# Layer 0's shifts and scales computed on the matmul array, and layer 1's modulation vectors moved from head 0 to heads 1 to 3

## The chip, the cores and the metric

One core of a Trainium2 chip runs the program. A core has five engines that work side by side and meet through semaphores: TensorE (PE in the rows, the matmul array, with its weight loads as PEld), VectorE (DVE), ScalarE (ACT), GpSimd (POOL) and SyncE (SP, which here only issues DMAs). The metric is the device time of one execution in microseconds (us); less is better.

## What is computed

A two-layer backbone over 512 latent tokens and 256 context tokens, 1024 features wide. Each layer is a normalised, modulated, gated residual step:

```
mod = silu(c) @ ada_w[i] + ada_b[i]          # shift, scale, gate: 3 x 1024, one set for c, one for c_ctx
h   = rms_norm(x, norm_g[i]) * (1 + scale) + shift
x   = x + gate * mixer(h)
```

The mixer of layer 0 is a bidirectional chunkwise mLSTM with four heads: projections to q, k (256 each per head), v, o, z (512 each per head) and four gates per head, a decay-weighted attention, a division by a denominator, `sigmoid(o) * normed * silu(z)`, and an output projection. The mixer of layer 1 is windowed attention over a band of 128 positions and the context. Layer 0 needs shift, scale and gate for both `c` (latent tokens) and `c_ctx` (context tokens); layer 1 needs shift and scale for both and the gate for `c` alone.

## The kernel before

Features lie on the 128 partitions (eight blocks j of 128) and tokens run along the free dimension (512 latent, then 256 context). Every large product is made in fp32r with operands split into a rounded part and a remainder (`hi`, `lo`), in three passes: `whi`x`hi`, `whi`x`lo`, `wlo`x`hi`. The rounded part comes from a ScalarE copy, the remainder from a subtraction on VectorE or GpSimd (`split`, L107).

The program's phases, in order of time:

- **Start.** 36 matmuls on zeros while x is loaded (`warm`), squares on ScalarE and their sums over the array (`pst`), and `rstd` (`rs`, L268).
- **The loop over the eight blocks j** (L313 to L371). For each block x is multiplied by `rstd` (L348, GpSimd), the modulation is applied by ScalarE (`enter`, L285: Identity with a scale and a bias per partition, which it reads from `modc`), the result is split into `HL` and `HC` (L288 on ScalarE, L289 on GpSimd), and TensorE then adds the block's share to the q and k of head 0 (`pqk`) and to all gates (`pgate`). So j's matmuls need j's shift and scale in `modc`.
- **Where shift and scale come from before.** `dots` (L206) multiplies a 128x1024 block of `ada_w` by silu(c) or silu(c_ctx), both broadcast over the partitions in `c2`, and sums along the row: one VectorE instruction for each block, part and vector, then a read of the accumulator. The eight scales and the shifts of blocks 0 and 4 to 7 are made so; the shifts of blocks 1 to 3 are made on the array (L328, then three transposes, L337).
- **Head 0.** Scores (`psc`), the gates' scans on VectorE (`gates`, L391 to L431), then the projections o and z (`po`, `pz`) interleaved with the decay weights and denominators (`decay`: L497 to L567, with `pden` at L520) and with modulation vectors (`mods`), in an order written by hand in the string `HEAD0`: o is a step of o and z, d a step of the decay, m one modulation vector. Then v (`v_proj`, `pv`), and the attention product (`ppv`).
- **Modulation vectors in head 0.** `todo` lists 32 vectors: layer 0's gate (8 blocks), then layer 1's shift, scale and gate (24). Each loads 512 KB and makes two dots (one for layer 1's gate). For the first eight the dot with `c_ctx` is a GpSimd multiplication (L210) and a ScalarE sum (L211). All 32 are done in head 0.
- **Heads 1 to 3** repeat q, k, scores, gates' weights, v, attention and o and z, with head h-1's output projection (`pwo`) between. In these heads o and z run last, from the end of `ppv`.

Tiles come from pools of fixed buffers; a new tile waits for the last reader of the buffer that it takes over. Within what the code and its `issue_after` marks fix, a scheduler sets each engine's order; each engine then works strictly in that order.

Of the kernel before, what the change touches and what calls it, by code (L numbers as in the profile page):

```python
# [16 lines left out]
P = 128  # L17
# [48 lines left out]
def hybrid_kernel(ctx: ExitStack, tc: tile.TileContext, a: dict, out: bass.AP, dbg=None):  # L68
# [50 lines left out]
    c2 = vga[:, 0:2048].rearrange("p (v k) -> p v k", v=2)  # L119
    crow = t0([P, 1792], F32, "pb")  # L120
    stage = [vga[:, 2048:3072]] + [vgb[:, 1024 * i : 1024 * i + 1024] for i in range(3)]
    qkp = t0([P, 6144], F32, "qkp")
    stage += [qkp[:, 1024 * i : 1024 * i + 1024] for i in range(2)] + [t0([P, 1024], F32, "qkt")]
    loaded = [0]

    def ada0(j, part):
        st = stage[loaded[0] % 7]
        loaded[0] += 1
        sy.dma_start(st, a["ada"][0, j, :, part])
        return st  # L130

    ccol = t0([P, KT, 2], F32, "ccol")
# [4 lines left out]
    small = [(crow[32 * v : 32 * v + 1, 0:D], a["cc"][v : v + 1]) for v in range(2)]  # L137
    small += [(ccol, a["cct"]), (adab, a["adab"]), (ng, a["ng"]), (hg, a["hg"]), (gb, a["gb"])]

    def load_x(small=()):  # L140
        xs = [t_([P, 4, T], F32, n) for n in ("xa", "xb")]
        for j in range(KT):
            sy.dma_start(xs[j // 4][:, j % 4], a["xin"][:, j])
            for dst, src in small[:2] if j == 0 else small[j + 1 : j + 2]:
# [4 lines left out]
    st0 = [ada0(0, 1), ada0(0, 0)]  # L149
# [9 lines left out]
    make_identity(nc, ident)  # L159
    tiny = t0([P, 1], F32, "tiny")  # L160
# [45 lines left out]
    def dots(layer, part, j, src, c2, vecs=(0, 1), pool=()):  # L206
        r = None
        for v in vecs:
            if v in pool:
                ge.tensor_mul(src, src, c2[:, v])  # L210
                se.activation(src, src, AF.Copy, accum_out=modc[:, layer, part, j, v : v + 1])  # L211
                continue
            junk = t0([P, 1024], BF16, "junk", 1)
            r = ve.tensor_tensor_reduce(
                out=junk, in0=src, in1=c2[:, v], scale=1.0, scalar=0.0,
                op0=ALU.mult, op1=ALU.add, accum_out=modc[:, layer, part, j, v : v + 1])
        return r
# [27 lines left out]
    for js in ((0, 1, 2, 3), (4, 5), (6, 7)):  # L245
        for j in js:
            q = tmp()
            lastsq = se.activation(q, x[j], AF.Square)
            if j == 1:
                for v in range(2):  # L250
                    r = crow[32 * v : 32 * v + 1, 0:D]
                    se.activation(r, r, AF.Silu)
                    ge.partition_broadcast(c2[:, v], r, channels=P)
            if j == 3:
                se.activation(ccol, ccol, AF.Silu)
# [7 lines left out]
    with after(*lastadd):  # L263
        lastdot = ve.tensor_scalar(bp1, adab[:, :, 1], 1.0, None, op0=ALU.add)
# [7 lines left out]
    with after(lastdot):  # L272
        dots(0, 1, 0, st0[0], c2, (0,))
        mod_fix(0, 1, 0, (0,))
        dots(0, 0, 0, st0[1], c2, (0,))
        mod_fix(0, 0, 0, (0,))
    rstd_exp, rstd_done = rs(0, TL, lastsq)
    xr_0 = tmp()
    xr0 = ve.tensor_mul(xr_0[:, 0:TL], x[0][:, 0:TL], rstd[:, 0:TL])
# [3 lines left out]
    def enter(j, v, xr, hf):  # L283
# [4 lines left out]
        hi = se.copy(dst[:, 0, j], hf[:, l:r])  # L288
        (ge if j or v else ve).tensor_sub(dst[:, 1, j], hf[:, l:r], f32(dst[:, 0, j]))  # L289
        return hi  # L290

    hf_0 = tmp()
    hi_0 = enter(0, 0, xr_0, hf_0)
    with after(xr0, hi_0):
        rs(TL, T)
        ve.tensor_mul(xr_0[:, TL:T], x[0][:, TL:T], rstd[:, TL:T])
        dots(0, 1, 0, st0[0], c2, (1,))
        mod_fix(0, 1, 0, (1,))
        dots(0, 0, 0, st0[1], c2, (1,))
        mod_fix(0, 0, 0, (1,))  # L300

    wgt = t0([P, 2048], F32R, "s")
# [3 lines left out]
    with after(rstd_exp):  # L306
        split(raw, wgt[:, 0:1024], wgt[:, 1024:2048], se, ge)
    half = big("pshift")
    acc = [big("pqk") for _ in range(3)]
    pg = ch("pgate")  # L310
    wq = [[None, None], [None, None]]
    stn = []
    for j in range(KT):  # L313
        if j == 0:
            for k in range(4):
                stn.append(qkp[:, 2048 + 1024 * k : 2048 + 1024 * k + 256 * NJ].rearrange("p (k c) -> p k c", k=2))
                sy.dma_start(stn[k], a["adan"][k])
        if j % 4 == 0:
            for u in range(2):
                with after(rstd_exp, *([xr0] if j or u else [])):  # L320
                    wq[u][j // 4] = load_w(a["w0"][0, u, j // 4], None if j or u else ge,
                                           raw=t0([P, 1024], F32, "pb") if u and not j else None)
        if j == 0:
            with after(laststat):
                warm(half, WARM2)

            for k in range(KT):
                te.matmul(half[0:2, 0 : P * NJ], ccol[:, k], stn[k // 2][:, k % 2], start=(k == 0), stop=(k == KT - 1))  # L328
            rows = t0([P, TL], F32, "bc1")
            with after(xr0):  # L330
                dots(0, 1, 1, ada0(1, 1), c2, (0,))
                lastdot = dots(0, 1, 1, stage[(loaded[0] - 1) % 7], c2, (1,))
                mod_fix(0, 1, 1)
            with after(rstd_exp):
                se.copy(rows[0:2, 0 : P * NJ], half[0:2, 0 : P * NJ])
                for i in range(NJ):
                    te.transpose(half[:, TL + 2 * i : TL + 2 * i + 2], rows[0:2, i * P : (i + 1) * P], ident[0:2, 0:2])  # L337
            with after(lastdot):
                for i in range(NJ):
                    ve.tensor_scalar(modc[:, 0, 0, 1 + i], half[:, TL + 2 * i : TL + 2 * i + 2],  # L340
                                     adab[:, 0, 0, 1 + i : 2 + i], None, op0=ALU.add)
        for part in (1, 0) if j > NJ else (1,) if j > 1 else ():
            with after(xr0):
                dots(0, part, j, ada0(j, part), c2)
                mod_fix(0, part, j)
        if j:
            xr, hf = tmp(), tmp()
            ge.tensor_mul(xr, x[j], rstd)  # L348
            enter(j, 0, xr, hf)
            enter(j, 1, xr, hf)  # L350
        else:
            enter(0, 1, xr_0, hf_0)
        st, sp = j == 0, j == KT - 1
        hl, hc = hparts(j)
        wgj = (wg[0][:, j], wg[1][:, j])
        wj = [[[wq[u][j // 4][m][:, j % 4, f * P : (f + 1) * P] for m in range(2)] for f in range(2)] for u in range(2)]
        mm3((pg[:, 0:TL],), wgj, [hl], st, sp)
# [3 lines left out]
        if j == 0:  # L361

            for u in range(2):
                with after(laststat):
                    te.matmul(acc[2][:, u * TL : (u + 1) * TL], zeror, wgt[:, 0:TL], start=True, stop=False)
        for u in (1, 0):
            for f in range(2):
                for i, (wi, m) in enumerate(PASSES):
                    te.matmul(acc[2][:, u * TL + f * TC : u * TL + (f + 1) * TC], wj[u][f][wi], hc[m],
                              start=False, stop=sp and f == 1 and i == 2)  # L370
        mm3((pg[:, TL:T],), wgj, [hc], st, sp)  # L371
# [11 lines left out]
    evac(1, True)  # L383

# [213 lines left out]
    def v_proj(h, vv):  # L598
# [9 lines left out]
        for c in range(4):  # L608
            w = ws[c]
            for n in range(6):  # L610
# [4 lines left out]
                if c == 3:  # L615
                    split(acc[n], vv[0][:, n], vv[1][:, n])
            if c < 2:
# [108 lines left out]
    vgb = t0([P, 3072], F32, "vgb")  # L726
    stage = [vga[:, 2048:3072]] + [vgb[:, 1024 * i : 1024 * i + 1024] for i in range(3)]

    def mods(n):
        for _ in range(min(n, len(todo))):  # L730
# [4 lines left out]
            dots(layer, part, j, st, c2, range(nv), pool=(1,) if len(todo) > NPOOL else ())  # L735

    def mods_fix():
        for layer, part, nv in ((0, 2, 2), (1, 0, 2), (1, 1, 2), (1, 2, 1)):
# [5 lines left out]

    xa = t_([P, 4, T], F32, "xa")
# [18 lines left out]
    stage = [vga[:, 2048:3072], t0([P, 1024], F32, "pb")]  # L764
    vgb = t0([P, 3072], F32R, "vgb")
    vv = [t_([P, 6, 512], F32R, "xb"), vgb.rearrange("p (t e) -> p t e", t=6)]
    vp = v_proj(0, vv)
    for n in MV:
        next(vp)
        mods(n)  # L770
    run(vp)
    mods(len(todo))
    H, norm = pv(vv, *pl, s)

    def gate0():
# [8 lines left out]
        mods_fix()  # L784


    for h in range(1, NH0):
# [13 lines left out]
        next(vp)  # L801
        next(dec)
# [14 lines left out]
        run(o_z(h, gated, pre, lambda: normalise(*norm)))  # L817
# [407 lines left out]
def layout(inp):  # L1225
# [74 lines left out]
```

## Time and profile before

| | |
|---|---|
| median of three runs | 1245.92 us (1245.25 to 1247.76) |
| the profiled execution | 1247.21 us |
| its span, first to last instruction | 1245.4 us |
| mean granted TensorE clock | 0.971 of full speed |
| PE busy | 1159.6 us, 93% |
| DVE / ACT / POOL busy | 820.4 / 548.8 / 304.8 us |

The profiled execution takes 1.3 us more than the median, and 1.8 us of it lie outside the span. PE is the engine with the least room: 86 us of the span are without a matmul, and a clock of 0.971 means that it ran at half speed for some part of the rest. The busy shares by slice show both losses mostly in the first quarter of the span: there the digits of PE are 7 and 8, behind it 9.

### The profile page before, as it was taken

The numbers are of one execution on the slowest core, as the hardware profiler recorded it, in microseconds if no ns is written. First come the engines' busy times: TensorE is split into PE (matmuls) and PEld (weight loads), VectorE is DVE, ScalarE is ACT, GpSimd is POOL, SyncE is SP. The second block draws the span as 40 slices with busy tenths as digits, with TensorE's granted clock in tenths as the row PEclk, the third lists the DMA queues.
The fourth block names the chain that finished last, engine by engine and source line by source line (L and its number), as shares of the span: only waits on it lengthen the run. The fifth ranks groups of instructions, "written<-read, shape, count | busy, mean of one in ns | idle before, by whom it ended". The sixth has DMA issues, their size and how long they took to land. (4 is left out here: it accounts for less than half of the span.)

```text
span 1245.4 us, 15926 instructions
## 1 busy us (share of the span) xinstructions
PE 1159.6 (93%) x6213; PEld 976.1 (78%) x6213; DVE 820.4 (66%) x1203; ACT 548.8 (44%) x913; POOL 304.8 (24%) x235
## 2 busy tenths in 40 slices
PE   7778698899999999999999999999999799998997
PEld 4666587687877888877888887788999587877776
DVE  6979798978672533366163148254777478989876
ACT  6324552333433422333423234343475377766663
POOL 3860770014301200420120222020043213223220
PEclk9788899999999999999999999999999899999999
DMA  8411643564211112121022211103205914124002
GB/s 305 169 51 34 203 130 115 158 217 161 87 54 34 49 67 68 64 76 51 18 81 68 68 47 64 51 20 121 81 20 119 220 51 119 56 81 122 32 18 68
DMA packets 38000, 112.71 MB, mean 90 GB/s; under 512 B 5027, under 2 KB 9251, under 8 KB 37413
## 3 DMA queue, kind: packets, MB, share of 16 engines
q1 hardware_dynamic: 35108, 104.35, 25.8%
q0 software_dynamic: 2816, 7.34, 3.4%
q8 instruction: 49, 0.80, 0.3%
q14 instruction: 27, 0.21, 0.1%
HBM read 103.42 MB, written 8.26 MB: 90 GB/s over the span
## 5 line engine op out<-in xcount | busy, mean ns | idle before, releaser
L103 ACT CAST whi<-wraw 128x1024 fp32r<-128x1024 f32 x102 | 106.9, 1051 | 198.3 <-PE pwo L189 43.8
L109 POOL TENSOR_TENSOR wlo<-wraw,whi 128x1024 fp32r<-128x1024 f32 x32 | 81.0, 2538 | 249.9 <-ACT whi L103 239.8
L109 DVE TENSOR_TENSOR wlo<-wraw,whi 128x1024 fp32r<-128x1024 f32 x70 | 89.2, 1275 | 60.9 <-ACT whi L103 60.7
L189 PE MATMUL pz<-HL,whi 128*128 128x512 f32 x256 | 96.3, 399 | 0.0
L189 PE MATMUL po<-HL,whi 128*128 128x512 f32 x256 | 96.0, 399 | 0.0
L189 PE MATMUL pqk<-HL,whi 128*128 128x512 f32 x256 | 94.3, 408 | 0.2 <-ACT whi L103 0.2
L189 PE MATMUL pv<-whi,HL 128*128 128x512 f32 x256 | 86.4, 405 | 5.1 <-DVE vgb L109 2.8
L189 PE MATMUL pz<-HC,whi 128*128 128x256 f32 x256 | 72.1, 282 | 0.0
L189 PE MATMUL po<-HC,whi 128*128 128x256 f32 x256 | 72.0, 281 | 0.0
L641 POOL TENSOR_TENSOR tmp<-tmp,tmp 128x768 f32<-128x768 f32 x8 | 15.9, 1984 | 228.4 <-ACT tmp L640 228.4
L189 PEld LDWEIGHTS pv<-whi,HL 128*128 128x128 f32 x256 | 49.8, 196 | 17.4 <-DVE vgb L109 4.2
L189 PE MATMUL Lq<-HL,whi 128*128 128x512 f32 (+1 forms) x192 | 56.1, 372 | 6.0 <-DVE szt L1068 6.0
L189 PEld LDWEIGHTS pqk<-HL,whi 128*128 128x128 f32 x256 | 49.9, 195 | 13.1 <-ACT whi L103 0.7
L189 PE MATMUL pqk<-HL,wlo 128*128 128x512 f32 x128 | 53.6, 419 | 6.9 <-DVE wlo L109 5.1
L1136 PE MATMUL Lpv<-PT,V 128*128 128x512 f32 x144 | 54.3, 431 | 5.7 <-DVE PT L109 4.5
L189 PEld LDWEIGHTS pz<-HL,whi 128*128 128x128 f32 x256 | 48.8, 190 | 12.4
L189 PEld LDWEIGHTS po<-HL,whi 128*128 128x128 f32 x256 | 48.5, 190 | 12.3
L1101 DVE TENSOR_REDUCE negm<-Lsc 128x2 f32<-128x1024 f32 (+1 forms) x32 | 43.4, 1355 | 15.7 <-PE Lsc L1099 15.2
L189 PE MATMUL pqk<-HC,whi 128*128 128x256 f32 x192 | 53.6, 279 | 0.0
L109 DVE TENSOR_TENSOR PT<-LT,PT 128x512 fp32r<-128x512 f32 x72 | 48.9, 684 | 4.8 <-ACT PT L103 4.2
L109 DVE TENSOR_TENSOR qkp<-pqk,qkp 128x768 fp32r<-128x768 f32 (+2 forms) x20 | 15.8, 794 | 54.7 <-ACT qkp L103 54.7
L189 PE MATMUL pz<-HL,wlo 128*128 128x512 f32 x128 | 51.7, 404 | 0.0
(386 smaller groups left out, 3399.1 us busy)
## 6 DMA issues: line engine op xcount, KB each, us to landing
wraw<-w SPq DMA_DIRECT2D x84, 512.0 KB, 3.6
wraw<-wo SPq DMA_DIRECT2D x24, 512.0 KB, 3.6
vga<-ada SPq DMA_DIRECT2D x16, 512.0 KB, 3.7
vgb<-ada SPq DMA_DIRECT2D x15, 512.0 KB, 4.9
pb<-ada SPq DMA_DIRECT2D x9, 512.0 KB, 3.7
Q<-hl POOLq DMA_DIRECT2D x8, 512.0 KB, 6.3
xa<-xin SPq DMA_DIRECT2D x8, 384.0 KB, 4.6
xb<-xin SPq DMA_DIRECT2D x8, 384.0 KB, 5.3
```

The lines of the kernel that those rows point to most:

```text
L103: se.copy(dst, src)
L109: return (le or ve).tensor_sub(lo, src, f32(hi))
L189: te.matmul(o, w[s], mv[m], start=first and i == 0, stop=last and i == 2)
L641: (ge if e < 3 else ve).tensor_add(ss, ss, sq)
L1101: ve.tensor_reduce(nmx[:, 0, 2 * p2 : 2 * p2 + 2], both, axis=AX.X, op=ALU.max, negate=True)
L1136: te.matmul(po, V[:, kb, g], hl[:, m], start=(bi == 0 and m == 0), stop=(bi == len(blocks) - 1 and m == 1))
```

## The change

Layer 0's shifts and scales all come from the array (`mod_quarter`): one quarter is 256 features of shift and of scale, that is two blocks j. `ada_w`'s part is laid out on the host as `ada0`, 16 loads of 512 KB. Each quarter is eight fp32 matmuls of 32 columns of weights and 512 moving columns, four of them in the array's four groups of 32 columns (output partitions 0, 32, 64, 96), the second four added on top. ScalarE copies the result, four tiny matmuls with the selector `sel2` add the four groups and turn the rows into columns, and three small VectorE operations add the bias and the norm's gain.

```
+    def mod_quarter(R, srcs, c):
+        for kk in range(2):
+            for g in range(4):
+                te.matmul(R[32 * g : 32 * g + 32], ccol[:, 4 * kk + g], srcs[4 * kk + g], start=kk == 0, stop=kk == 1)
+        rt = tmp()[:, 0:TL]
+        se.copy(rt, R)
+        for q in range(4):
+            te.matmul(R[:, 2 * q : 2 * q + 2], rt[:, q * P : (q + 1) * P], sel2, start=True, stop=True)
...
     for j in range(KT):
+        if j % 2 and j < KT - 1:
+            c = j // 2 + 1
+            with after(lastmm):
+                mod_quarter(R[:, c % 2 * TL : c % 2 * TL + TL], st0[c], c)
+        xr, hf = tmp(), tmp()
+        ve.tensor_mul(xr, x[j], rstd)
+        enter(j, 0, xr, hf)
+        enter(j, 1, xr, hf)
...
-        mm3((pg[:, 0:TL],), wgj, [hl], st, sp)
...
+    pg = ch("pgate")
+    for j in range(KT):
+        mm3((pg[:, 0:TL], pg[:, TL:T]), (wg[0][:, j], wg[1][:, j]), hparts(j), j == 0, j == KT - 1)
```

The multiplication by `rstd` and the subtractions of `HL` and `HC` are on VectorE now, and GpSimd has nothing to do in the loop. The gates' matmuls stand behind the loop. 36 and 8 warming matmuls (36 and 10 before); the eight stand among the statistics.

In head 0 only layer 0's gate remains, with both dots on VectorE. The 24 vectors of layer 1 are done in heads 1 to 3, in the stage of o and z:

```
-HEAD0 = "ooodommoommmmmomoddmmmmm"
-MV = (0, 2, 2, 3, 3)
-NPOOL = 24
+HEAD0 = "ooodommommommommodd"
+MODS = (None, (3, 3, 2, 2), (3, 3, 2, 2), (4, 0, 0, 0))
...
+    def mods_at(rows, slots):
+        nonlocal c2, stage
+        c2 = rows.rearrange("p (v k) -> p v k", v=2)
+        sy.dma_start(rows, c_d.rearrange("r k -> (r k)").partition_broadcast(P))
+        stage = slots
...
+        rows = t0([P, 6144], F32, "qkp")
+        mods_at(rows[:, 0:2048], [rows[:, 1024 * i : 1024 * i + 1024] for i in range(2, 6)])
+        for n, _ in zip(MODS[h], o_z(h, gated, pre, lambda: normalise(*norm))):
+            mods(n)
+    mods_fix((1, 0, 2), (1, 1, 2), (1, 2, 1))
```

`c2` now comes from DRAM: silu(c) is turned into rows on the array, written out (`c_d`) and read back by every partition, 1 MB each time, for head 0 and again for each of heads 1 to 3. In heads 1 to 3 the vectors' buffers are the q and k buffer `qkp`, which `ppv` has to have read first.

**TensorE, between block 0 and block 1.** `R` is the accumulator of the quarters, `tmp_313` its copy, `pqk_222` the context part of q and k. Before:

```order
L369 MATMUL pqk_228<-HC_202,whi_236 128x256 x2
L369 MATMUL pqk_228<-HC_202,wlo_237 128x256
L189 MATMUL pgate_229<-HC_202,s_220 128x256 x3
L189 MATMUL pgate_229<-HL_201,s_220 128x512 x3
L189 MATMUL pqk_226<-HL_201,whi_236 128x512 x2
```

Now:

```order
L331 MATMUL pqk_222<-HC_218,whi_234 128x256 x2
L331 MATMUL pqk_222<-HC_218,wlo_235 128x256
L221 MATMUL R_199<-vgb_67,ccol_71 32x512 x4
L221 MATMUL R_199<-qkp_68,ccol_71 32x512 x4
L225 MATMUL R_199<-sel_109,tmp_313 128x2 x4
L192 MATMUL pqk_220<-HL_217,whi_234 128x512
L192 MATMUL pqk_221<-HL_217,whi_240 128x512
```

Block 1's first matmul stands directly behind the second quarter, with nothing between them; the third quarter stands so behind block 2, and the fourth behind block 4, there with nine of the gates' matmuls behind it.

**GpSimd, in head 0's decay.** `tmp_805` and `tmp_791` gather the sums for the denominator that `pden` waits for. Before:

```order
L537 COPY tmp_805<-pb_798 128x128
L535 TENSOR_TENSOR tmp_805<-pb_798 128x512
L536 TENSOR_TENSOR tmp_805<-pb_798,s_734 128x128
L210 TENSOR_TENSOR vgb_796<-vgb_796,vga_66 128x1024
L545 TENSOR_TENSOR tmp_805<-tmp_805,s_734 128x128
L545 TENSOR_TENSOR tmp_805<-tmp_805,s_734 128x256
L210 TENSOR_TENSOR vgb_796<-vgb_796,vga_66 128x1024
L545 TENSOR_TENSOR tmp_805<-tmp_805,s_734 128x384
L546 TENSOR_TENSOR tmp_805<-tmp_805,pb_798 128x512
```

Now:

```order
L508 COPY tmp_791<-pb_784 128x128
L506 TENSOR_TENSOR tmp_791<-pb_784 128x512
L507 TENSOR_TENSOR tmp_791<-pb_784,s_718 128x128
L516 TENSOR_TENSOR tmp_791<-tmp_791,s_718 128x128
L516 TENSOR_TENSOR tmp_791<-tmp_791,s_718 128x256
L516 TENSOR_TENSOR tmp_791<-tmp_791,s_718 128x384
L517 TENSOR_TENSOR tmp_791<-tmp_791,pb_784 128x512
```

The modulation's multiplications (L210) no longer stand between the sums.

**VectorE, in head 1's stage of o and z.** `wlo` is the remainder of half a unit of weights, `junk` the unused product of a dot. Before:

```order
L810 SCALAR_TENSOR_TENSOR pb_2872<-pb_2872,s_2186 128x768 x2
L109 TENSOR_TENSOR wlo_3132<-wraw_3129,whi_3131 128x1024
L689 SCALAR_TENSOR_TENSOR tmp_3068<-tmp_3068,pz_3019 128x768
L814 SCALAR_TENSOR_TENSOR tmp_3068<-tmp_3068,hg_74,pb_2872 128x768
L109 TENSOR_TENSOR vgb_2531<-tmp_3068,vga_2530 128x768
L109 TENSOR_TENSOR wlo_3138<-wraw_3135,whi_3137 128x1024
```

Now:

```order
L785 SCALAR_TENSOR_TENSOR pb_2751<-pb_2751,s_2063 128x768 x2
L212 ISA junk_3031,modc_113<-qkp_2749 128x1024
L212 ISA modc_113 128x1
L106 TENSOR_TENSOR wlo_3041<-wraw_3038,whi_3040 128x1024
L662 SCALAR_TENSOR_TENSOR tmp_2962<-tmp_2962,pz_2913 128x768
L212 ISA junk_3034,modc_113<-qkp_2749 128x1024
L212 ISA modc_113 128x1
L789 SCALAR_TENSOR_TENSOR tmp_2962<-tmp_2962,hg_74,pb_2751 128x768
L212 ISA junk_3036,modc_113<-qkp_2749 128x1024
L212 ISA modc_113 128x1
L106 TENSOR_TENSOR vgb_2408<-tmp_2962,vga_2407 128x768
L106 TENSOR_TENSOR wlo_3047<-wraw_3044,whi_3046 128x1024
```

The rows of the remainders now have dots between them: since the stage began, ten stand ahead of the first of these two and twelve ahead of the second, where there were none.

## Rows read from the trace of the kernel before

**Rows 1.** Busy time in stretches: stretch, length, us and (times) by engine, PEclk.
```profile
140.00:160.00 20.00, 8.61 (x35) 7.24 (x34) 19.96 (x19) 7.27 (x12) 17.77 (x10) 0.66 0.40 126
...
sum 320.00, PE 272.36 PEld 221.64 DVE 273.37 ACT 128.93 POOL 129.32; mean PE 17.02 PEld 13.85 DVE 17.09 ACT 8.06 POOL 8.08
```

**Rows 2.** ACT's waits, 0 to 100 us: line, releaser, total, times, longest.
```profile
ACT tmp L285 <- DVE modc L224: 25.4, 4, 8.3
ACT tmp L285 <- DVE modc L222: 11.9, 3, 6.6
```

**Rows 3.** PE's waits, 0 to 400 us, same columns.
```profile
PE pden L520 <- ACT tmp L103: 13.8, 2, 11.4
...
PE pv L189 <- DVE xb L689: 3.5, 2, 2.3
...
PE pv L189 <- DVE vgb L109: 2.8, 1, 2.8
PE psc L189 <- ACT qkp L103: 2.8, 2, 2.2
...
PE pwo L189 <- DVE vgb L109: 1.6, 2, 1.2
```

**Rows 4.** Two lines' instructions: duration in ns (min/median/max), first and last start.
```profile
L328 PE MATMUL pshift<-qkp,ccol x16: 485/486/486, 19.7 to 24.5; 128*2 128x384 f32 x16
...
L214 DVE CUSTOM_DVE_ANT_0 junk<-vgb,vga x25: 1211/1226/3307, 17.2 to 191.7; 128x1024 bf16<-128x1024 f32 x25
```

**Rows 5.** Groups in the loop, 30 to 96 us: shapes, count, total, mean ns.
```profile
L285 ACT ACTIVATE tmp<-tmp,modc 128x512 f32<-128x512 f32 x7 | 5.7, 815 | 37.3 <-DVE modc L224 25.4 <-DVE modc L222 11.9
L288 ACT CAST HL<-tmp 128x512 fp32r<-128x512 f32 x7 | 4.2, 603 | 0.0
```

**Rows 6.** TensorE's timeline: start, length, instruction, idle before and its releaser.
```profile
71.20 0.79 PE L189 MATMUL pqk<-HL,wlo 128*128 128x512 f32 x1 [4.24 <-DVE wlo L109]
...
95.34 0.52 PE L189 MATMUL pgate<-HC,s 128*128 128x256 f32 x3
...
111.67 0.39 PE L189 MATMUL po<-HL,whi 128*128 128x512 f32 x1
111.90 0.28 PE L189 MATMUL po<-HC,whi 128*128 128x256 f32 x1
112.01 0.40 PE L189 MATMUL po<-HL,whi 128*128 128x512 f32 x1
...
115.20 0.87 PE L435 MATMUL pgt<-ident,vgb 64*128 64x64 f32 x6 [2.32 <-DVE vgb L419]
...
154.09 1.01 PE L520 MATMUL pden<-tmp,onesr 128*128 128x512 f32 x2 [11.39 <-ACT tmp L103]
```

**Rows 7.** Stretches behind gaps of TensorE, columns as in rows 1.
```profile
30.00:43.00 13.00, 8.05 (x22) 6.22 (x23) 12.86 (x18) 3.72 (x7) 8.71 (x5) 0.50 0.66 243
...
70.00:74.00 4.00, 2.79 (x9) 2.41 (x10) 3.96 (x7) 2.04 (x4) 3.13 (x3) 0.61 0.44 133
...
204.00:208.00 4.00, 3.02 (x12) 2.17 (x12) 3.96 (x5) 0.00 (x0) 0.00 (x0) 1.00 0.53 139
```

**Rows 8.** GpSimd in head 0's decay, start and length.
```profile
140.62 2.44 POOL L210 TENSOR_TENSOR vgb<-vgb,vga 128x1024 f32<-128x1024 f32 x1
...
151.05 2.12 POOL L546 TENSOR_TENSOR tmp<-tmp,pb 128x512 f32<-128x512 f32 x1
```

**Rows 9.** VectorE, first decay multiplication of head 0, and one of head 1's remainders.
```profile
134.27 3.52 DVE L503 SCALAR_TENSOR_TENSOR pb<-tmp,ebcol,s 128x640 f32<-128x640 f32 x3 [1.20 <-ACT tmp L497]
...
433.57 1.23 DVE L109 TENSOR_TENSOR wlo<-wraw,whi 128x1024 fp32r<-128x1024 f32 x1
```

**Rows 10.** Head 1's stage of o and z: stretch, and TensorE's use of a remainder.
```profile
400.00:440.00 40.00, 40.00 (x226) 34.60 (x225) 22.02 (x19) 17.14 (x18) 7.53 (x4) 1.00 0.17 52
440.00:480.00 40.00, 40.00 (x228) 34.68 (x227) 14.14 (x14) 12.47 (x16) 0.00 (x0) 1.00 0.20 65
...
441.51 0.40 PE L189 MATMUL po<-HL,wlo 128*128 128x512 f32 x1
```

More of the change, by code (lines that the diff above doesn't have):

```diff
@@ L118, in hybrid_kernel @@
     vga, vgb = t0([P, 3072], F32, "vga"), t0([P, 3072], F32, "vgb")
-    c2 = vga[:, 0:2048].rearrange("p (v k) -> p v k", v=2)
-    crow = t0([P, 1792], F32, "pb")
-    stage = [vga[:, 2048:3072]] + [vgb[:, 1024 * i : 1024 * i + 1024] for i in range(3)]
     qkp = t0([P, 6144], F32, "qkp")
[L123 to L132, printed above, removed]
+    stage = [v[:, 1024 * i : 1024 * i + 1024] for v, n in ((vga, 3), (vgb, 3), (qkp, 6)) for i in range(n)]
+    stage.append(t0([P, 1024], F32, "qkt"))
+    csil = t0([P, 2, KT], F32, "csil")
+    ccol = t0([P, KT, 32], F32, "ccol")
     adab = t_([P, 2, 3, KT], F32, "adab")
@@ L148, in hybrid_kernel, with ada0 @@
     _, x = load_x(small)
-    st0 = [ada0(0, 1), ada0(0, 0)]
+    loaded = [0]
+    def ada0(c):
+        r = []
+        for i in range(4):
+            st = stage[loaded[0] % len(stage)]
+            loaded[0] += 1
+            sy.dma_start(st, a["ada0"][c, i])
+            r += [st[:, 0:TL], st[:, TL : 2 * TL]]
+        return r
+    st0 = [ada0(0)]
+    ge.memset(ccol, 0.0)
     ones = t0([P, P], F32, "ones")
@@ L270, in rs @@
         return rsqrt(rstd[:, l:r], v_[:, l:r], y_[:, l:r], w_[:, l:r], prev)
[L272 to L279, printed above, removed]
+    rstd_exp, _ = rs(0, TL, lastsq)
+    rs(TL, T)
+    R = ch("R")
+    mod_quarter(R[:, 0:TL], st0[0], 0)
     HL = t_([P, 2, KT, TL], F32R, "HL")
@@ L287, in enter @@
         dst = (HL, HC)[v]
[L288 to L302, printed above, removed]
+        split(hf[:, l:r], dst[:, 0, j], dst[:, 1, j])
+    wgt = t0([P, 3072], F32R, "s")
+    acc = [big("pqk") for _ in range(3)]
+    pbw = t0([P, 1024], F32R, "pb")
+    warm(acc[0], WARM2)
+    wq = [[load_w(a["w0"][0, u, 0]), None] for u in range(2)]
+    st0.append(ada0(1))
+    wq[0][1] = load_w(a["w0"][0, 0, 1])
+    st0.append(ada0(2))
+    raw = t_([P, 1024], F32, "wraw", 2)
+    sy.dma_start(raw, a["w0"][0, 1, 1])
+    split(raw, wgt[:, 2048:3072], pbw)
+    wq[1][1] = [w.rearrange("p (k c) -> p k c", k=4) for w in (wgt[:, 2048:3072], pbw)]
+    st0.append(ada0(3))
     wg = [wgt[:, i * 1024 : (i + 1) * 1024].rearrange("p (k c) -> p k c", k=KT) for i in range(2)]
@@ L305, in hybrid_kernel @@
     sy.dma_start(raw, a["wg"])
[L306 to L312, printed above, removed]
-    for j in range(KT):
[L314 to L352, printed above, removed]
@@ L383, in hybrid_kernel @@
     evac(1, True)
+    pt = ch("pct")[0:16, 0:P]
+    te.transpose(pt, csil.rearrange("p v k -> p (v k)"), ident)
+    se.copy(crow, pt)
+    sy.dma_start(c_d, crow)
     negM_d = dr.tile([64, T], F32, name="negM_d")
@@ L725, in hybrid_kernel @@
     todo = [(0, 2, j, 2) for j in range(KT)] + [(1, p, j, 2 if p < 2 else 1) for p in range(3) for j in range(KT)]
-    vgb = t0([P, 3072], F32, "vgb")
-    stage = [vga[:, 2048:3072]] + [vgb[:, 1024 * i : 1024 * i + 1024] for i in range(3)]
+    c2 = stage = None
+    def mods_at(rows, slots):
[3 more added lines that the diff above has]
+        stage = slots
     def mods(n):
@@ L734, in mods, with mods_fix @@
             sy.dma_start(st, a["ada"][layer, j, :, part])
-            dots(layer, part, j, st, c2, range(nv), pool=(1,) if len(todo) > NPOOL else ())
-    def mods_fix():
-        for layer, part, nv in ((0, 2, 2), (1, 0, 2), (1, 1, 2), (1, 2, 1)):
+            dots(layer, part, j, st, c2, range(nv))
+    def mods_fix(*what):
+        for layer, part, nv in what:
             m = modc[:, layer, part, :, 0:nv]
@@ L743, in mods_fix @@
                 ve.tensor_mul(m, m, ng[:, layer, :, None].to_broadcast([P, KT, nv]))
+    vga, vgb = t0([P, 3072], F32, "vga"), t0([P, 3072], F32, "vgb")
+    mods_at(vga[:, 0:2048], [vga[:, 2048:3072]] + [vgb[:, 1024 * i : 1024 * i + 1024] for i in range(3)])
     xa = t_([P, 4, T], F32, "xa")
@@ L763, in hybrid_kernel @@
             first = []
-    stage = [vga[:, 2048:3072], t0([P, 1024], F32, "pb")]
     vgb = t0([P, 3072], F32R, "vgb")
     vv = [t_([P, 6, 512], F32R, "xb"), vgb.rearrange("p (t e) -> p t e", t=6)]
[L767 to L772, printed above, removed]
+    run(v_proj(0, vv))
     H, norm = pv(vv, *pl, s)
@@ L801, in hybrid_kernel @@
         next(vp)
+        next(vp)
         next(dec)
```

67 lines of the change are left out of this document (30 added, 37 removed).

## The prediction, made before the change was run

> **What bounds the kernel now.** I read the busy time by stretch first. Over the first 320 us TensorE is busy for 272.4 [rows 1], so 47.6 us of the 86 without a matmul lie here, in a quarter of the span. The stretches behind its gaps show a second loss: from 30 to 43 us the granted clock is 0.50 (the 1.2 GHz level), from 70 to 74 it is 0.61 [rows 7]. From 400 to 480 TensorE is busy without a gap at full clock [rows 10]. A gain can come from the first 320 us alone, and heads 1 to 3 have only something to lose.
>
> The waits say what is late there. In the loop over j, ScalarE's Identity waits 25.4 + 11.9 us for the modulation constants [rows 2], that is for VectorE's dots; one takes 1.23 us in the median and up to 3.3 [rows 4]. TensorE then waits for what follows. Behind the loop TensorE waits 2.8 us for q and k, once 11.4 us at `pden`, and 3.5 + 2.8 us in v [rows 3]. At `pden` the late one is the decay: GpSimd's multiplications for the modulation (2.44 us) stand between its sums [rows 8], and dots stand between VectorE's multiplications.
>
> **Price of a quarter's products.** The array's shifts before are the nearest row: 16 passes of 384 columns in 19.7 to 24.5 us, 0.32 us a pass, two passes for one fp32 matmul [rows 4]. At 512 columns that is 0.43 us a pass, by estimate. A quarter has eight matmuls, 16 passes. Call their time X. No row shows matmuls in different column groups beside each other, so I bound it. If they follow one another, X = 16 x 0.43 = 6.8 us. If all four groups run side by side, a quarter of that, 1.7, and some 1.9 with the start of the last. If starts keep the order of the program and the two passes of one matmul share a group, only the second pass of one and the first of the next can overlap: nine steps, X = 9 x 0.43 = 3.8. I take 3.8: it needs nothing but the order in which the rows of the queue stand.
>
> The Trainium skill ("TensorE: Matmul & The Clock Gate", Part 3, Packing small matmuls) measured 2.38 times for three column groups at 512 columns, and says that matmuls start and end in program order. By 2.38 X would be about 2.9 us, and the sum below 3 us better. The same skill ("TensorEngine Tiling (Array Packing)", Tiling Modes, Key Properties) says that a change of the tiling mode drains the array, which speaks against this change eight times over; no row of this trace shows a price for it.
>
> **The loop.** Behind each quarter comes a chain that TensorE waits out: ScalarE's copy of 512 columns (0.60, as the cast of that width), Identity of 512 columns 0.82 and the cast 0.60 [rows 5]; by estimate four tiny matmuls 0.4, three small VectorE operations 0.7, the Identity of 256 columns 0.5 and 0.3 of hand-overs: 3.9 us. Before the first block it all starts where the array's shifts started, at 19.7 [rows 4], and gives 19.7 + 3.8 + 4.1 = 27.6 for the first real matmul. One block's share of q and k is 12 passes of 512 and 12 of 256 columns. The starts at 111.67, 111.90 and 112.01 give 0.23 and 0.12 a pass [rows 6], so 4.2 us at full clock. Block 0 I price at half clock, 8.4, as from 30 to 43 before [rows 7]: end 36.0. Seven blocks at 4.2: 29.4. Three quarters at 3.8 + 3.9: 23.1. VectorE's and ScalarE's own work for a block (2 to 3 us each, by estimate from the same rows) lies under the matmuls.
>
> The clock is the next term. Before, the gap of 4.2 us that ends at 71.20 [rows 6] is followed by a stretch at 0.61, and gaps of about 2.3 us around 204 are followed by one at 1.00 [rows 7]. The chain of 3.9 is near the first, so behind the second and third quarter I expect some 4 us at the low level, 1.9 lost each, 3.8. The fourth has nine of the gates' matmuls under its chain. End of q and k: 36.0 + 29.4 + 23.1 + 3.8 = 92.3. The gates' 38 matmuls left at a mean 0.175 add 6.6: 98.9, where the loop ended at about 95.9 (95.34 + 0.5) before [rows 6]. The scores took from there to 111.67, 15.8 us, with 2.8 of waits for q and k [rows 3] and a restart in pieces. Now the gates' tail covers the splitting of q and k, and 10 us remain. Head 0's first `po` stands at 108.9 instead of 111.67: **gain 2.8**.
>
> **Head 0.** The gates' scans run under the scores, and they now start 10 us ahead of `po` instead of 15.8. The stall at `pgt` (2.32 [rows 6]) grows to about 4. From the end of the gates' matmuls to the first decay multiplication at 134.27 [rows 9] were 38.4 us; the splits that shared VectorE are done earlier now, so I take 36.5, which is 26.5 behind `po` (22.6 before). From there to `pden` at 154.09 were 19.8. The decay's own VectorE work, without GpSimd beside it, is about 6; two dots lie in it (2.5), then GpSimd's last two sums (3) and the cast (0.8): 12. `pden` stands 38.5 behind `po`, 42.4 before: **gain 3.9**. TensorE still runs dry for some 6 us ahead of it, so I expect the half clock behind it to stay.
>
> In v the waits of 3.5 + 2.8 us [rows 3] are for `xb` and `vgb` operations that stand behind dots; with 24 of 32 vectors gone no dot is left there. A restart at the low level belongs to them: 4 us at 0.61 lost 1.6 elsewhere [rows 7], I count 1.2. **Gain 7.5**. The waits of `pwo`, 1.6 [rows 3], go for the same reason: **gain 1**.
>
> **Heads 1 to 3.** 20, 16 and 4 dots move in, at 1.25 us with the read of the accumulator 50 us of VectorE work, where TensorE has no slack. VectorE is busy 22 of the 40 us from 400 and 14 of the next 40 [rows 10], so they fit by volume. They do not quite fit by order: twelve dots (15 us) stand ahead of the remainder that VectorE made at 433.57 [rows 9] and TensorE reads at 441.51 [rows 10]. Its end at 434.8 leaves 6.7 us; the dots can fill some 10 us in which VectorE stood idle, so 5 us of them push: 1.7 us to spare. The broadcast of `c_d` waits for `ppv` and stands in SP's queue ahead of three loads of vectors that wait for dots, and those ahead of the weights' load: this can eat the rest. **Loss 3** for all heads, between 0 and 9.
>
> **Sum.** 2.8 + 3.9 + 7.5 + 1 - 3 = 12.2. The profiled execution took 1247.2 (span 1245.4), so 1235.0 for one like it; it is 1.3 above the median, so I forecast 1233.8 against 1245.92, rounded to **1234**.
>
> **Rivals.** (a) *Four groups side by side.* X = 1.9 and not 3.8: four quarters save 1.9 each, 7.6 less a part that the loads of weights take back at the start; 6. Time 1228. For it: the groups have their own columns and partitions. Without the losses of clock and of the heads it would be 1222. (b) *The groups follow one another.* X = 6.8: three quarters cost 9 more and the start 2.5, 11.5 in all. Time 1245.5, no change. For it: no row shows an overlap, and the 16 passes of the shifts before stood in a strict row [rows 4]. (c) *Heads 1 and 2 pay, and the kernel is slower.* The gain without the heads is 15.2. There are 40 dots, 36 of them in heads 1 and 2, and one that stands bare between a weight's cast and its remainder delays TensorE by 1.25. From 13 bare dots (16) on the gain is gone, and at 18 bare dots (22) the time is 1253. SP's queue is what could do this, since weights behind blocked loads come late for every unit of the stage; against it stand 1.7 us of room at the tightest remainder. (d) *The stalls move.* If the decay waits for DMA or ScalarE as long as for GpSimd before, and v waits for the normal chain, the 11.4 us of head 0 shrink to 4: 1241.
>
> **How the numbers follow.** Forecast (X near 3.8) 0.42; (a) 0.28; (d) 0.13; (b) 0.09; (c) 0.08. Only (c), half of (b) and a corner of (d) lie at 1243.4 or above, 0.2% below the median, which is about what a measurement of this kernel can tell from no change. So faster 0.82, same 0.08, slower 0.10. The range runs from 1222, case (a) without the other losses, to 1246, case (b); (c) and the far corners are left out.
>
> **What would show it.** The quarters' rows of the changed kernel: starts 0.43 apart in pairs (3.8), four almost together (1.9), or 16 in a row (6.8). The loop: first `po` at 109 us; at 103 (a) holds, at 120 (b). The granted clock behind the second and third quarter: below 0.7, or the 3.8 were not lost. `pden` 38 us behind `po`, with a wait near 6. No waits of v on `xb` and `vgb`. In heads 1 and 2, TensorE's waits for `wlo` and `whi` in the stage of o and z: none or up to 3 us, where (c) wants more than 15. I am wrong if the first `po` comes later than 114 or heads 1 to 3 take over 9 us more.

## The result and the profile after

The changed kernel takes 1207.97 us (median of four runs, 1205.80 to 1208.84) against 1246.16 for the kernel before: a ratio of 0.969, with a 95% interval from 0.9673 to 0.9706. That is 38 us less. The forecast was 12 less, and its range ended at 1222: the direction was right, the size was far too small.

Where the time went is read best from a few landmarks. Each time is the first start of the named matmuls, or the last of `pz`, in the two profiled executions (1247.21 and 1208.84 us):

| landmark | before | forecast | after | lead, forecast | lead, measured |
|---|---|---|---|---|---|
| first block's `pqk` (`pgate` before) | 26.9 | 27.6 | 27.5 | -0.7 | -0.6 |
| first score behind the gates' matmuls | 96.4 | 98.9 | 87.8 | -2.5 | 8.6 |
| head 0's first `po` | 111.7 | 108.9 | 97.7 | 2.8 | 14.0 |
| head 0's first `pden` | 154.1 | 147.4 | 137.2 | 6.7 | 16.9 |
| first `pwo`, in head 1 | 296.2 | 282.0 | 269.9 | 14.2 | 26.3 |
| last `pz`, end of head 3 | 880.2 | 868.0 | 841.5 | 12.2 | 38.7 |
| end of the span | 1245.4 | 1233.2 | 1207.0 | 12.2 | 38.4 |

The lead at `po` is 11 us larger than forecast. Between `po` and `pwo` the forecast nearly held (11.4 against 12.3). Behind it, where the sum had a gain of 1 at `pwo` and a loss of 3 in heads 1 to 3, come 12.4.

TensorE's waits from 0 to 400 us, with the columns of [rows 3] (engine, what waits, for whom, total, times, longest):

```profile
PE pden L491 <- ACT tmp L100: 5.4, 2, 5.2
PE pqk L192 <- ACT HL L100: 5.2, 3, 3.9
PE pgt L406 <- DVE vgb L390: 4.0, 1, 4.0
PE R L225 <- ACT tmp L223: 2.8, 4, 0.7
```

The 11.4 us at `pden` of [rows 3] are 5.2, and v's waits for `xb` and `vgb` are gone. What is left at the top is what a quarter makes TensorE wait for, the gates' chain, and the shorter wait at `pden`. The stretches of 20 us, with the columns of [rows 1]:

```profile
20.00:40.00 20.00, 14.00 (x78) 8.93 (x74) 11.22 (x22) 10.33 (x18) 0.00 (x0) 0.79 0.91 354
...
60.00:80.00 20.00, 18.81 (x115) 15.11 (x114) 5.72 (x12) 7.44 (x15) 3.49 (x2) 1.00 0.23 79
...
sum 320.00, PE 297.77 PEld 245.66 DVE 191.84 ACT 132.23 POOL 63.34; mean PE 18.61 PEld 15.35 DVE 11.99 ACT 8.26 POOL 3.96
```

TensorE is busy 297.8 of the first 320 us, where [rows 1] had 272.4; VectorE falls from 273 to 192 and GpSimd from 129 to 63.

The quarter's products answer the price that no row of before could give. TensorE's timeline of the changed kernel, second quarter, read at four starts (start, length, instruction, count from that start on), and then the end of its chain:

```profile
34.36 0.64 PE L221 MATMUL R<-vgb,ccol 128*32 128x512 f32 x4
...
34.82 0.61 PE L221 MATMUL R<-vgb,ccol 128*32 128x512 f32 x4
...
35.25 0.61 PE L221 MATMUL R<-qkp,ccol 128*32 128x512 f32 x4
...
35.67 0.61 PE L221 MATMUL R<-qkp,ccol 128*32 128x512 f32 x4
...
36.99 1.05 PE L225 MATMUL R<-sel,tmp 128*128 128x2 f32 x8 [0.70 <-ACT tmp L223]
38.70 1.22 PE L192 MATMUL pqk<-HL,whi 128*128 128x512 f32 x2 [0.66 <-ACT HL L100]
```

Four passes start together, every 0.43 us. Sixteen passes end at 36.3, 1.9 us after the first began. The next block's matmuls then start at 38.70, 2.4 us behind the products and not 3.9.

### The profile page after: what moved, and what is told of

Read it like the earlier page. It is cut to its first block, busy times and chain, and to the rows that moved or that the text cites. A ratio compares the mean times of both kernels' runs of the same rounds, so it can differ in the third digit from the quotient of the medians.

```text
span 1207.0 us, 15997 instructions
## 1 busy us (share of the span) xinstructions
PE 1151.3 (95%) x6289; PEld 972.6 (81%) x6289; DVE 766.9 (64%) x1184; ACT 541.1 (45%) x901; POOL 230.1 (19%) x203
## 5 line engine op out<-in xcount | busy, mean ns | idle before, releaser
L106 POOL TENSOR_TENSOR wlo<-wraw,whi 128x1024 fp32r<-128x1024 f32 x31 | 75.3, 2436 | 278.5 <-ACT whi L100 269.6
L192 PE MATMUL pqk<-HL,whi 128*128 128x512 f32 x240 | 90.3, 410 | 5.6 <-ACT HL L100 5.2
L192 PE MATMUL pv<-whi,HL 128*128 128x512 f32 x256 | 83.1, 391 | 0.0
L192 PEld LDWEIGHTS pqk<-HL,whi 128*128 128x128 f32 x240 | 46.1, 195 | 18.0 <-ACT HL L100 5.5
L192 PEld LDWEIGHTS pz<-HL,whi 128*128 128x128 f32 x256 | 48.5, 190 | 12.4
L212 DVE CUSTOM_DVE_ANT_0 junk<-qkp 128x1024 bf16<-128x1024 f32 x40 | 48.7, 1218 | 5.1 <-DMA qkp<-ada 4.6
L192 PE MATMUL po<-HL,wlo 128*128 128x512 f32 x128 | 51.8, 405 | 0.0
```

The lines of the kernel that those rows point to most:

```text
L106: return (le or ve).tensor_sub(lo, src, f32(hi))
L192: te.matmul(o, w[s], mv[m], start=first and i == 0, stop=last and i == 2)
L212: ve.tensor_tensor_reduce(out=junk, in0=src, in1=c2[:, v], scale=1.0, scalar=0.0, op0=ALU.mult, op1=ALU.add, accum_out=modc[:, layer, part ...
```

## Experiments

Each run is told with its median, and with the ratio to the kernel before that was run on the same chip.

**One more step in v's projection, alone, in the kernel before.** The change has three lines that neither the section on the change nor the sum took up. They move no work to another engine, only one meeting point:

```
-MV = (0, 2, 2, 3, 3)
+MV = (0, 0, 2, 2, 3, 3)
...
             for n in range(6):
                 ...
+                if c == 0 and n == 1:
+                    yield
...
         next(vp)
+        next(vp)
         next(dec)
```

The added 0 in `MV` is of this run alone: it keeps head 0's vectors where they were.

> The kernel before with one edit: v's projection gives way once more, after the first two of its six token tiles, so that in heads 1 to 3 the second denominator stands 12 matmuls later in TensorE's order. Theory (this step alone made the gain of heads 1 to 3): the waits at the second denominator of heads 1 to 3, 2.4 us each, and the half clock behind them, about 1.6 each, go: 12 us less, 1234. Rival (heads 1 to 3 gained because head 0 no longer makes layer 1's vectors, or from VectorE's relief): no change, 1246 within 1.

Measured: 1237.65 us, ratio 0.9933 (0.9905 to 0.9962), 8 us less. TensorE's waits from 240 to 860 us, first of the kernel before, then of this one:

```profile
PE pden L520 <- ACT tmp L103: 7.3, 3, 2.4
```

```profile
PE pden L520 <- DVE tmp L109: 1.1, 3, 0.4
PE pden L520 <- ACT tmp L103: 0.6, 3, 0.2
```

Three waits of 2.4 us at the second denominator became 1.7 us in all. The granted clock, 0.96 in the stretches of 40 us from 520 and from 720 of the kernel before, is 1.00 there in this run. With 12 more matmuls of v ahead of it, the sums are there when TensorE asks. In the profiled runs heads 1 to 3 (first `pwo` to last `pz`) took 573.6 us instead of 584.0. The theory holds; the price was 8 by the medians and 10 in the profiled runs, not 12.

**The same step taken out of the changed kernel.**

```
-                if c == 0 and n == 1:
-                    yield
...
-        next(vp)
         next(vp)
         next(dec)
```

> The changed kernel without the additional step in v's projection. Theory: the same 12 us come back, 1220, and the waits at the second denominator of heads 1 to 3 are 2.4 us again. Rival: 1208 within 1.5.

Measured: 1216.05 us (1212.33 to 1219.95), ratio 0.9752; 8 us come back and not 12, and with them the waits, in the same stretch:

```profile
PE pden L491 <- ACT tmp L100: 7.4, 3, 2.5
```

The step is worth about 8 us in either kernel.

**A quarter's products in one column group.**

```
-te.matmul(R[32 * g : 32 * g + 32], ccol[:, 4 * kk + g], srcs[4 * kk + g], start=kk == 0, stop=kk == 1)
+te.matmul(R[0:32], ccol[:, 4 * kk + g], srcs[4 * kk + g], start=kk + g == 0, stop=kk + g == 4)
...
-        se.copy(rt, R)
+        se.copy(rt[0:32], R[0:32])
...
-te.matmul(R[:, 2 * q : 2 * q + 2], rt[:, q * P : (q + 1) * P], sel2, start=True, stop=True)
+te.matmul(R[:, 2 * q : 2 * q + 2], rt[0:32, q * P : (q + 1) * P], sel2[0:32], start=True, stop=True)
```

> All eight products of a quarter go to the first group of 32 columns and add up there. Theory (the four groups run side by side, and that is what makes a quarter 1.9 us long): 16 passes of 0.43, 6.8 us a quarter, 4.9 more each; three quarters lie bare between blocks and the first ahead of block 0, so 15 to 20 us more, 1223 to 1228, and first po at 112 to 117 us instead of 97.7. Rival (a product with 32 columns of weights is short by itself, or the loop isn't on the path): 1208 to 1211.

Measured: 1231.16 us, ratio 0.9872 (0.985 to 0.9895): 23 us more than the changed kernel, with the first `po` at 121.2. TensorE's timeline at the third quarter, and its stretch behind the gap, with the columns of [rows 7]:

```profile
59.27 7.05 PE L221 MATMUL R<-qkp,ccol 128*32 128x512 f32 x16
66.99 1.05 PE L225 MATMUL R<-sel,tmp 32*128 32x2 f32 x8 [0.66 <-ACT tmp L223]
68.71 0.73 PE L192 MATMUL pqk<-HL,whi 128*128 128x512 f32 x2 [0.67 <-ACT HL L100]
```

```profile
68.00:73.00 5.00, 3.91 (x11) 2.92 (x11) 3.91 (x9) 3.08 (x7) 0.00 (x0) 0.66 0.02 5
```

Sixteen passes take 7.05 us in one group where they took 1.9 in four: the groups are worth a factor of 3.7. The time is above the 15 to 20 expected. Of the 23.5 us at the first `po`, the third and the fourth quarter make 5.1 each. The start makes 2.5 only, since in the changed kernel the first block waited beyond its quarter's products (see below). The second quarter makes 7.5: behind its products the gap is 4.8 us here and not 2.4, because the next block's multiplication by `rstd` stood behind the quarter's operations on VectorE. The other 3 us are mostly the clock, which is low behind all three later quarters here (0.66 each time). The same third quarter of the changed kernel, behind the same two gaps of 0.7 us:

```profile
53.00:58.00 5.00, 4.34 (x22) 3.53 (x23) 3.69 (x7) 3.01 (x7) 0.00 (x0) 1.00 0.02 5
```

There the granted clock stays at 1.00. Behind the second quarter it doesn't in this execution. The stretch of 5.9 us behind that gap, first in the changed kernel, then in the run without the step, whose loop is the same:

```profile
38.70:44.60 5.90, 5.90 (x24) 4.80 (x25) 4.68 (x8) 4.16 (x7) 0.00 (x0) 0.72 0.56 222
```

```profile
36.80:42.70 5.90, 5.46 (x28) 4.54 (x29) 4.69 (x8) 3.60 (x7) 0.00 (x0) 1.00 0.65 260
```

So the same loop has a low stretch in one execution and none in another, and its first `po` stands at 97.7 or, as in the run without the step, at 94.9.

**Both products of one group behind one another.**

```
-        for kk in range(2):
-            for g in range(4):
+        for g in range(4):
+            for kk in range(2):
```

> The changed kernel with the eight products of a quarter in another order: both products of one column group, then the next group's. Theory (TensorE starts its matmuls in the order of its queue, and side by side run only those of different groups that stand behind one another): two groups overlap at each change of group only, 13 steps of 0.43, 5.6 us a quarter and not 1.9, 3.7 more for each: 11 to 15 us more, 1219 to 1223. Rival (a matmul starts when its group is free, whatever stands ahead of it): 1.9 us a quarter, 1207 to 1209.

Measured: 1208.04 us, against 1206.30 for the changed kernel on the same chip: no difference that can be told. My theory falls. In the code a product of `vgb` and one of `qkp` alternate now, in the second quarter. The trace has them in another order (timeline, two reads):

```profile
32.69 0.66 PE L221 MATMUL R<-vgb,ccol 128*32 128x512 f32 x4
...
33.57 1.06 PE L221 MATMUL R<-qkp,ccol 128*32 128x512 f32 x8
```

All eight passes of `vgb` start first, four by four, then all of `qkp`. The trace doesn't hold the queue's order itself. That it did change shows in the starts of one set of four, 13 to 14 ns apart here and 6 to 7 in the changed kernel, as if another product stood between each two. Read so, a matmul in a free column group starts ahead of one that stands before it in the queue and has to wait for its own group, and the sentence on the kernel before that each engine works strictly in its order doesn't hold for TensorE's matmuls.

**Layer 1's vectors back in head 0.**

```
-HEAD0 = "ooodommommommommodd"
-MODS = (None, (3, 3, 2, 2), (3, 3, 2, 2), (4, 0, 0, 0))
+HEAD0 = "ooodommoommmmmomoddmmmmm"
+MV = (0, 0, 2, 2, 3, 3)
+MODS = (None, (0, 0, 0, 0), (0, 0, 0, 0), (0, 0, 0, 0))
...
-    run(v_proj(0, vv))
+    vp = v_proj(0, vv)
+    for n in MV:
+        next(vp)
+        mods(n)
+    run(vp)
+    mods(len(todo))
```

> The changed kernel with layer 1's 24 vectors made in head 0 again, at the places of the kernel before, all dots on VectorE. Theory (head 0's v stage was late because of these dots): the waits of v on xb and vgb come back, 7 to 10 us, and heads 1 to 3 give back at most 2: 1213 to 1217. Rival (40 dots cost heads 1 to 3 as much as they cost head 0): 1206 to 1210.

Measured: 1218.12 us, ratio 0.9768 (0.9746 to 0.9789), 10 us more, just above the 1213 to 1217 expected. TensorE's waits from 150 to 300 us:

```profile
PE ppv L606 <- DVE vgb L107: 2.4, 3, 1.3
PE pv L193 <- DVE xb L663: 2.2, 1, 2.2
PE pv L193 <- DVE vgb L107: 1.9, 2, 1.1
PE pwo L193 <- DVE vgb L107: 1.3, 1, 1.3
```

v waits for `xb` and `vgb` again, 4.1 us where it was 6.3 in the kernel before, and so does `pwo` (1.3 us; 1.6 before). The 2.4 us in `ppv` are new. The first `pwo` is 8.8 us later than in the changed kernel, and the last `pz` 11.7: a further 2.9 us are lost in heads 1 to 3, where this kernel has no dots at all.

**Without layer 1's vectors.**

```
-MODS = (None, (3, 3, 2, 2), (3, 3, 2, 2), (4, 0, 0, 0))
+MODS = (None, (0, 0, 0, 0), (0, 0, 0, 0), (0, 0, 0, 0))
...
-        mods_at(rows[:, 0:2048], [rows[:, 1024 * i : 1024 * i + 1024] for i in range(2, 6)])
```

> The changed kernel without layer 1's 24 modulation vectors: neither their loads nor their dots nor the broadcasts of c_d in heads 1 to 3 (layer 1 then works with zeros for its constants). Theory (heads 1 to 3 hide the 40 dots under TensorE's work): 1206 to 1209, TensorE's waits in the stages of o and z as without them. Rival (they cost the 3 us of the prediction, or up to 9): 1199 to 1205.

Measured: 1207.35 us (1205.73 to 1212.18), ratio 0.9711. The 40 dots cost heads 1 to 3 nothing that can be measured. In the changed kernel TensorE has no gap in head 1's stage of o and z, in which VectorE is busy 55 of 66 us:

```profile
369.60:436.00 66.40, 66.40 (x378) 57.61 (x377) 54.57 (x69) 24.41 (x26) 6.81 (x3) 1.00 0.45 149
```

**GpSimd's share of the loop given back to it.**

```
-        split(hf[:, l:r], dst[:, 0, j], dst[:, 1, j])
+        split(hf[:, l:r], dst[:, 0, j], dst[:, 1, j], se, ge if j or v else ve)
...
-        ve.tensor_mul(xr, x[j], rstd)
+        (ge if j else ve).tensor_mul(xr, x[j], rstd)
```

> The changed kernel with the multiplication by rstd and the remainders of HL and HC on GpSimd, as before, for the blocks behind the first. Theory (GpSimd's three operations of a block, 2.7 + 1.8 + 1.6 us in the kernel before, are longer together than a block's 4.2 us on TensorE): seven blocks at 6.1 instead of 4.2 or a little more, less what the quarters' gaps cover: 8 to 14 us more, 1216 to 1222. Rival (GpSimd's work hides, and the dots alone made the loop slow): 1208 to 1210.

Measured: 1210.31 us (1210.19 to 1211.71), 2 us more than the changed kernel by the medians and 4 by the ratios; the theory of 8 to 14 falls. Its premise was the length of GpSimd's operations before, and they are shorter now. GpSimd's groups in the loop (shapes, count, total, mean ns, idle), first of the kernel before from 30 to 96 us, then of this one from 20 to 90:

```profile
L289 POOL TENSOR_TENSOR HC<-tmp,HC 128x256 fp32r<-128x256 f32 x8 | 13.1, 1636 | 0.0
...
L348 POOL TENSOR_TENSOR tmp<-xb,bc 128x768 f32<-128x768 f32 x4 | 11.3, 2835 | 0.0
```

```profile
L314 POOL TENSOR_TENSOR tmp<-xb,bc 128x768 f32<-128x768 f32 x4 | 7.3, 1826 | 0.0
L106 POOL TENSOR_TENSOR HC<-tmp,HC 128x256 fp32r<-128x256 f32 x8 | 7.1, 888 | 26.3 <-ACT HC L100 26.3
```

The same multiplication takes 1.83 us instead of 2.84 once VectorE makes no dots beside it. It need not be a dot. The subtraction for `HC`, 1.64 in the mean before, takes 0.75 in the last block of the kernel before, where VectorE has nothing to do; in this run one takes 1.77 while VectorE makes a remainder of weights (40.96 to 42.19). First the kernel before, then this run:

```profile
90.09 0.75 POOL L289 TENSOR_TENSOR HC<-tmp,HC 128x256 fp32r<-128x256 f32 x1
```

```profile
41.02 1.77 POOL L106 TENSOR_TENSOR HC<-tmp,HC 128x256 fp32r<-128x256 f32 x1
```

So most of the loop's gain comes from taking the dots away, not from relieving GpSimd.

**The chain of a quarter behind the next block's first matmuls.**

```
-        rt = tmp()[:, 0:TL]
+    def quarter_end(R, c):
+        rt = tmp()[:, 0:TL]
...
         for u in range(2):
             for f in range(2):
                 mm3((acc[u][:, f * TL : (f + 1) * TL],), wj[u][f], [hl], st, sp)
+            if u == 0 and j % 2 and j < KT - 1:
+                quarter_end(R[:, c % 2 * TL : c % 2 * TL + TL], c)
```

> The changed kernel with the second half of a quarter (ScalarE's copy, the four matmuls with the selector, VectorE's three operations) written behind the first half of the next block's matmuls, so that ScalarE takes that block's Identity first. Theory (the next block's constants come from the quarter before, and only ScalarE's order makes it wait): the gaps of 2.4 us behind the second and third quarter and the half clock behind the second go: 5 to 7 us less, 1201 to 1203. Rival (the chain is needed for the next block): no gain, 1208 or later.

Measured: 1200.16 us (1199.77 to 1203.85), ratio 0.9647 (0.9628 to 0.9667), 5 to 6 us less than the changed kernel by the ratios. Head 0's first `po` stands at 91.5, and the gaps of 2.4 us behind the second and third quarter are gone. Block 1 needs nothing of the second quarter: at j = 1 the quarter c = 1 is made, and it serves blocks 2 and 3. What held block 1 was ScalarE's copy, queued ahead of its Identity. This is the fastest version found; the two later runs that contain this edit lie within 2 us of it.

**Four steps of o and z ahead of head 0's first denominator.**

```
-HEAD0 = "ooodommommommommodd"
+HEAD0 = "oooodmmommommommodd"
```

> The changed kernel with one more step of o and z ahead of the first denominator of head 0 (HEAD0 with four o before the first d and one less behind). Theory (TensorE runs dry ahead of that denominator, 5.2 us and half clock behind it): 5 to 8 us less, 1200 to 1203. Rival (the wait comes back at the second denominator or in v): less than 2 us, 1206 to 1209.

Measured: 1205.20 us, ratio 0.9679; 2 us less than the changed kernel by the ratios, within the intervals. The wait at `pden` is gone, and two others stand behind it (TensorE's waits to 400 us):

```profile
PE pz L192 <- ACT whi L100: 3.0, 1, 3.0
...
PE pz L192 <- POOL wlo L106: 2.4, 1, 2.4
```

The stall moved to a weight whose cast stands behind a cast of the decay in ScalarE's queue: close to the rival's time, though not at the places that it named, and most of the gain was lost to it.

**Both edits together.** The last two edits in one kernel; then the changed kernel on that chip.

> The two edits that each gained something together: the second half of a quarter behind the next block's first matmuls, and four steps of o and z ahead of head 0's first denominator. Theory (they act in different stages): 7.8 + 2.8 less than the changed kernel, 1197 to 1198. Rival (head 0's wait for weights takes back what comes in earlier): 1200 to 1202.

> The changed kernel itself, on the chip of the next three, to compare them on one chip: 1206 to 1209.

Measured: 1201.80 us against 1206.30 for the changed kernel, 4.5 less; not the sum of both. The rival is right: the waits for weights in `pz` (2.7 and 2.4 us) are there again.

**The gates' matmuls in pairs behind blocks 4 to 7, with the covered chain.**

```
+        if j == 4:
+            pg = ch("pgate")
+        if j >= 4:
+            for jj in (2 * j - 8, 2 * j - 7):
+                with after(lastmm):
+                    mm3((pg[:, 0:TL], pg[:, TL:T]), (wg[0][:, jj], wg[1][:, jj]), hparts(jj), jj == 0, jj == KT - 1)
```

> The second half of a quarter behind the next block's first matmuls, and the gates' matmuls no longer all behind the loop: blocks 0 and 1 behind block 4, 2 and 3 behind block 5, and so on. Theory (head 0 waits for the gates' chain, which starts when the last of these matmuls ends, while the splitting of q and k then lies bare ahead of the scores): the scores wait 2 to 4 us, the stall at pgt (4.0) and the wait at the denominator (5.2) lose more than that: 1195 to 1199. Rival (what the chain gains the scores lose): 1199 to 1203.

Measured: 1201.73 us, no gain over 1200.16. The waits at `pgt` stayed at 4.1 in two pieces, that at `pden` at 5.7. The theory falls, and what sets the start of the gates' chain here I did not follow further.

**The array part alone.** The changed kernel with layer 1's vectors in head 0 and without the additional step:

```
-HEAD0 = "ooodommommommommodd"
+HEAD0 = "ooodommoommmmmomoddmmmmm"
+MV = (0, 2, 2, 3, 3)
...
-                if c == 0 and n == 1:
-                    yield
```

> Only the first part of the change: the quarters on the array (with GpSimd out of the loop and the gates behind it); layer 1's vectors are made in head 0 as before, and v's projection has no additional step. Theory (the three parts add up: 38.2 us in all, 8.3 for the step by the first of these runs, 10.1 for the vectors): 19.8 us less than the kernel before, 1224 to 1227. Rival (the parts cover one another, since less waiting in one stage lets a wait in the next grow): 1218 to 1222, or above 1230.

Measured: 1225.89 us, ratio 0.9846 (0.9825 to 0.9866), 19 us less than the kernel before. With 8.3 for the step and 10.1 for the vectors the sum is 37, of 38 measured: the three parts add up, within the 2 or 3 us to which each is known.

## Why the prediction was wrong, point by point

**What bounds the kernel.** Right for the first 320 us. Wrong in "heads 1 to 3 have only something to lose". I read the two stretches of o and z [rows 10], where TensorE is full, for the whole of three heads. The second denominators of these heads waited 7.3 us in the kernel before; the first row of [rows 3] already had 2.4 us beside the 11.4. The lines of the step stood in the change, and I priced neither them nor their place. By place this is the larger miss: a loss of 2 forecast behind the first `pwo`, 12.4 gained. The step is 8 to 10 of it by the first two runs, and about 3 come from the vectors that head 1 no longer has to finish. By parts of the change, the array's was to bring 6.7 (2.8 + 3.9) and brought 19, the vectors 5.5 (8.5 - 3) and 10, the step nothing and 8.

**Price of a quarter's products.** The step that failed is "starts keep the order of the program and the two passes of one matmul share a group". The groups start side by side, and by the run with the other order the queue's order does not hold across them. X is 1.9 and not 3.8: rival (a), with 0.28, was the true one here. Rival (b) was 17.5 us away from it in my sum (1245.5 against 1228); its run shows 23.

The Trainium skill ("TensorE: Matmul & The Clock Gate", Part 3, Packing small matmuls) gives 2.38 for three groups; four groups gave 3.7 here (7.05 to 1.9 us). It says there that matmuls start in program order; the run with the other order shows starts that do not, if the queue has the order of the code there. Of the drain at a change of mode ("TensorEngine Tiling (Array Packing)", Tiling Modes, Key Properties) the trace shows little: the last matmul of the block before it started at 34.15, the next at its pace of 0.12 would have started at 34.27, and the first product starts at 34.36, 0.1 us later.

**The loop.** The chain of 3.9 us was an error in reading the change: I let block 1 wait for the second quarter, but its constants come from the first. The gap is 2.4, by ScalarE's order alone, and the run with the covered chain removed it. Half clock cost less too: block 0 took 6.9 us, not 8.4, and of the three quarters only the second was followed by the low level in the profiled execution (5.9 us for a block of 4.2), and in others of the same loop none. Together: 3 x 1.9 for X, 3 x 1.5 for the chain, 1.5 and 2.1 for the clock, 13.8. Against it, the ten matmuls of the gates under the fourth quarter's chain did not lie under it but behind it, 1.8, and a block waited for a remainder, 0.8. That leaves 11.2 of the 11.1 measured. That the first block started as forecast, at 27.5 against 27.6, is luck: its quarter took 1.9 us less, but from there to the first real matmul passed 5.7 us and not 4.1, about 1 us of it because on ScalarE a cast of weights (1.03 us) stood ahead of the cast of `HL`.

**Head 0.** The scores took 9.9 us (10 forecast), the stall at `pgt` 4.0 (about 4), the wait at `pden` 5.2 (some 6), and `pden` came 39.5 us behind `po` (38.5). From `pden` to the first `pwo` 9.4 us were gained (7.5); the 1 us of `pwo`'s own waits lies behind its first start. These steps were right, and the run with the vectors in head 0 confirms the cause in v: the waits come back with the dots.

**Heads 1 to 3, the dots.** The loss of 3 did not come: the run without them is not faster. The bound of 9 and rival (c) rested on SP's queue and on VectorE's order; TensorE had no gap in those stages (busy 66.4 of 66.4 us in head 1, 65 of 65 from 575 us in head 2, 62 of 62 from 780 us in head 3). Rival (d) had a true core only in later edits: a stall that is removed at `pden` comes back at a weight.

**The range.** It took in (a) without losses, 1222. It could not hold 1208, because no case in it gave heads 1 to 3 a gain. With a part of the change left without a price, the bounds of the priced parts could not hold the time.

## What to carry to other kernels

Price every line of a diff, also those that move only a meeting point in a hand-written order: three lines here were worth a fifth of the whole, and the wait that they removed stood in the waits of the kernel before. Before a wait is priced, find which earlier product serves it: a result that is made a block ahead costs only what its copies hold up in another engine's queue. Small matmuls in different column groups ran side by side in both orders tried, so a quarter's eight products took eight dots from VectorE for 1.9 us of TensorE, and 2.4 us of waiting until the next block's Identity went ahead of the copy.

## What the runs showed of the hardware that I had not expected

- Matmuls in four column groups of 32 started within 20 ns of one another, and 16 passes of 512 columns took 1.9 us against 7.05 in one group; with the order in the code changed, the passes still started in the old order, all eight of `vgb` first.
- GpSimd's operations last longer beside VectorE's work: the same 128x768 multiplication took 2.84 us beside dots and 1.83 without, a 128x256 subtraction 0.75 alone and 1.77 beside a subtraction on VectorE.
- Behind 7 us of products in one group the granted clock fell at each of the three later quarters (0.66). Behind 1.9 us in four groups with gaps of 0.7 us it fell behind the second quarter of the changed kernel (0.72) and not in the run without the step (1.00), whose loop is the same. What decides this no run here shows.
